# Products with values of two pairs of heads given out together, in the two layers with heads of 64

## The chip, the cores and the metric

The kernel runs on one core of a Trainium2 chip, alone. The metric is the device time of one execution in microseconds (us); the time before is the median of three runs. The engines are named as the profile names them: PE is TensorE (matrix products), PEld its loads of weights, DVE VectorE, ACT ScalarE, POOL GpSimd, SP the engine that issues most transfers.

## The reference

A decoder trunk of four layers over 256 positions and 1024 features, in float32. Layer by layer it does:

```
h = x
for i in range(4):                       # mixers: differential, MoBA, sliding window, differential
    h = h + mixer(rms_norm(h, attn_norm_g[i]))
    h = h + (max(rms_norm(h, mlp_norm_g[i]) @ w_up[i], 0) ** 2) @ w_down[i]
return rms_norm(h, final_norm_g)
```

Each mixer projects to queries, keys and values, turns a quarter of each head by rotary tables, and takes a softmax over masked scores; the products of the probabilities with the values go through an output projection. The differential layers have 8 heads with values of 128. The MoBA layer (i = 1) has 16 heads of 64; with 256 positions it holds a single block, so it is plain causal attention. The sliding-window layer (i = 2) has 16 query heads of 64 over 2 heads of keys and values, a window of 128, a bias, and a sink term in the denominator. These last two are the layers with heads of 64.

## The kernel before, in words

All activations stay in SBUF, transposed, as four tiles hT of 128 x 512. The weights are streamed: one DMA of 1 MB brings a raw piece (`fetch`, L66), ACT copies it to a rounded tile whi (`stage`, L80), DVE subtracts to get the rest, wlo (L81). `take` keeps two pieces staged ahead and five fetched ahead. A product with full precision is then made of several passes over the high and low parts.

The projections into a mixer are `proj` (L296, tile p_in). The attention works on pairs of heads, eight pairs in each of the two layers. For a pair n the steps are, by the name that the kernel's plan gives them:

- QK: queries and keys of two pairs are transposed on PE (L461, p_qk), and split into high and low parts by ACT (L470, L477) and DVE (L471, L478).
- SC: scores on PE (L271 to L273, tiles p_s0 and p_s1); masking with the row maximum on DVE (L336), exponentials on ACT (L339), in the sliding-window layer the sink terms (L342, L345); then the division by the sums (L424, L425, L427).
- TR: six transposes of the probabilities on PE (L354, p_t), brought to SBUF by ACT (L355, tile et).
- AV: the product with the values (L436, p_av). The two heads of a pair are two matrices of 64 columns, written to the two halves of one PSUM bank. This is four matmuls in the program and eight matmul instructions in the trace, each with its load of weights. ACT (L439) and DVE (L440) bring the result to the tile oo, in a high and a low part.

The output projection (p_d and p_e; L271 to L273 in the sliding-window layer, L605 and L606 in the MoBA layer) reads oo. PSUM tiles of the attention share four banks with the tag "wk", taken in turn: p_qk, p_s0, p_s1, p_t and p_av all rotate through them.

What sets the order: in the MoBA layer a written plan (L569 to L572), a list of thirteen entries; entry 2a is given out midway through projection a, entry 2a+1 after it, the last entry at the end. In the sliding-window layer the function `step` (L445): each call takes a new pair and advances the generators of the pairs in its line by one stage each. Whatever is given out is then placed by a scheduling layer, which may pull independent work, such as the matmuls of the output projection, between the steps; the order of the built program is what PE, ACT and DVE follow.

Of the kernel before, what the change touches and what calls it, by code (L numbers as in the profile page):

```python
# [39 lines left out]
def trunk(ctx: ExitStack, tc: tile.TileContext, xT, gains, lams, swa_row, fng, weights, out):  # L40
# [402 lines left out]
    line = []  # L443

    def step(block=None):  # L445

        line.append(block)
        full = len(line) > 3
        for x in line[:0:-1] + line[:1] if full else line[::-1]:
            if x is not None:  # L450
                next(x, None)
        if full:
            line.pop(0)

    def turn(src, n):

# [23 lines left out]
    def mixer_layer(i, n):  # L480
# [4 lines left out]
        if mixer == 2:  # L485
# [15 lines left out]
            for c in range(4):  # L501
                p = proj(n, (256, 1), False, first)
                qn = room(c % 2, [P, NT, 256], "qn")
                for t in range(NT):
                    for h in range(2):
                        s = slice(P * h, P * h + P)
                        o = qn[:, t, :].rearrange("p (b h e) -> p b h e", h=2, e=HD)[:, :, h, :]
                        bs = bias[:, 512 * h + P * c:512 * h + P * c + P]
                        V.scalar_tensor_tensor(o, p[t][:, s].rearrange("p (b e) -> p b e", e=HD), r[:, t:t + 1],
                                               bs.rearrange("p (b e) -> p b e", e=HD), op0=OP.mult, op1=OP.add)  # L510
                rope(qn[:, :, :].rearrange("p t (s e) -> p t s e", e=HD), 4)
                for do in second:
                    do()
                qs = []

                def block(b, c=c, qs=qs, qn=qn):
                    if b == 0:
                        qs += put_q(turn(lambda b, t: qn[:, t, P * b:P * b + P], 2))
                    h = 2 * c + b
                    step(head_block(  # L520
                        parts, [x[:, b] for x in qs], kT, lambda m: kv[:, m, P:2 * P], band,
                        [(sink[:, h + 8 * s:h + 8 * s + 1], nsink[:, h + 8 * s:h + 8 * s + 1]) for s in range(2)],
                        h,
                    ))

                first, second = [lambda f=block: f(0)], [lambda f=block: f(1)]
        else:
# [36 lines left out]
            def LAM(_):  # L564
                if i == 0:
# [1 line left out]

            order = (0, 1, "v", 2, 3, "v") if mixer else (0, 1, "v", 2, "v", 3)
            plan = [[], [], [(QK, 0), (LAM, 0), (SC, 0)], [(SC, 1)], [(TR, 0), (QK, 1), (SC, 2)], [(TR, 1), (SC, 3)],  # L569
                    [(TR, 2), (AV, 0)], [(TR, 3), (AV, 1)], [(AV, 2), (QK, 2), (OUT, 0), (SC, 4)], [(AV, 3), (SC, 5)],  # L570
                    [(TR, 4), (QK, 3), (OUT, 1), (SC, 6)], [(TR, 5), (SC, 7)],
                    [(AV, 4), (TR, 6), (AV, 5), (TR, 7), (AV, 6), (OUT, 2), (AV, 7), (OUT, 3)]]  # L572
            if mixer == 0:
                plan[8:] = [[(AV, 2), (QK, 2), (OUT, 0), (SC, 4)], [(AV, 3), (SC, 5)], [(TR, 4), (AV, 4)],
                            [(OUT, 1), (TR, 5), (AV, 5)],
                            [(QK, 3), (SC, 6), (SC, 7), (OUT, 2), (TR, 6), (AV, 6), (TR, 7), (AV, 7)]]
# [20 lines left out]
        for _ in range(3):  # L597
            step()
# [187 lines left out]
    for j in range(4):  # L786
        norm_sum(n, j)
    for i in range(DEPTH):
        parts, rest = mixer_layer(i, n)
        n = new_norm(gv[:, 1, i, :])  # L790
        (out_proj if i % 3 == 1 else out_proj_all)(parts, n, rest)
# [106 lines left out]
```

## Time and profile before

| | |
|---|---|
| median of 3 runs | 1148.51 us (1148.4 to 1148.52) |
| the profiled execution | 1148.08 us |
| its span, first to last instruction | 1146.0 us |
| mean granted TensorE clock | 0.998 |
| PE busy | 1135.6 us (99%) |
| PEld, DVE, ACT busy | 988.2, 827.8, 660.0 us |
| MoBA attention products (L436) | 64 matmul instructions, from 346.9 to 394.0 us |
| sliding-window attention products (L436) | 64 matmul instructions, from 623.4 to 657.3 us |

How to read it: a busy time is the union of an engine's instructions. Matmuls are pipelined, so each lasts longer than its share of the engine; what an instruction costs on PE is read from the distance between the starts of two neighbours. An "x8" in the timeline is a merged row of eight instructions.

### The profile page before, as it was taken

Reading aid. Unit: us, or ns where it says so; the run is one execution under the profiler, and the core shown is the slowest. Engines: PE = TensorE matmul, PEld = TensorE weight load, DVE = VectorE, ACT = ScalarE, POOL = GpSimd, SP = SyncE. Lnnn points to the kernel's source line nnn. Section 1 sums busy time; section 2 is a strip of 40 time slices with the busy share of each in tenths; the row PEclk is TensorE's granted clock in tenths of the full one; section 3 lists DMA queues with packets and bytes.
Section 4 is the critical chain, followed back from the end, with each engine's and each line's share of the span. In section 5 each row is a group of like instructions: output and inputs, shape, how many; then the busy total and the mean of one; then the engine's idle time right before and its main releaser. Section 6 shows DMA issues by size and latency. Waiting matters only on the chain.

```text
span 1146.0 us, 17054 instructions
## 1 busy us (share of the span) xinstructions
PE 1135.6 (99%) x6560; PEld 988.2 (86%) x6560; DVE 827.8 (72%) x1608; ACT 660.0 (58%) x1207; POOL 11.4 (1%) x39
## 2 busy tenths in 40 slices
PE   9999999999999999999999999999999999999997
PEld 7789888888887888888899898888888889888886
DVE  8978977656676698766569887775567788777454
ACT  6866656544476675554446756554447676665342
POOL 1000000000000000000000000000000000000000
PEclk9999999999999999999999999999999999999999
DMA  8543465555543355555563346555554444554551
GB/s 330 195 147 119 167 198 193 198 194 184 184 147 133 125 184 188 190 203 191 185 208 111 111 148 214 190 184 185 187 195 136 148 143 160 191 198 169 184 184 37
DMA packets 30609, 198.66 MB, mean 173 GB/s; under 512 B 3521, under 2 KB 5185, under 8 KB 7361
## 3 DMA queue, kind: packets, MB, share of 16 engines
q1 hardware_dynamic: 30240, 197.06, 50.2%
q8 instruction: 51, 0.84, 0.3%
q10 hardware_dynamic: 288, 0.52, 0.1%
q14 instruction: 30, 0.24, 0.1%
HBM read 196.52 MB, written 1.05 MB: 172 GB/s over the span
## 4 chain that ended last, share of the span: by engine, by line
PE 95%; DVE 2%; DMA 1%; ACT 1%; issue 0%; SPq 0%; DVEq 0%; ACTq 0%
PE p_up L605 20%; PE p_in L296 18%; PE p_down L605 15%; PE p_up L606 11%; PE p_down L606 8%; PE p_last L272 3%; PE p_last L271 3%; PE p_last L273 3%; PE p_d L272 2%; PE p_d L273 2%; PE p_d L271 2%; DMA raw<-in_weights 1%; PE p_t L354 1%; PE p_s L271 1%; PE p_qk L461 1%; PE p_av L436 1%
## 5 line engine op out<-in xcount | busy, mean ns | idle before, releaser
L81 DVE TENSOR_TENSOR wlo<-raw,whi 128x1024 fp32r<-128x1024 f32 (+1 forms) x374 | 447.2, 1209 | 204.1 <-ACT whi L80 203.3
L80 ACT ACTIVATE whi<-raw 128x1024 fp32r<-128x1024 f32 (+1 forms) x374 | 384.3, 1046 | 216.4 <-issue 111.1
L605 PE MATMUL p_up<-hg,whi 128*128 128x512 f32 x1024 | 356.7, 393 | 0.5 <-DVE hg L229 0.2
L606 PE MATMUL p_up<-hg,wlo 128*128 128x256 f32 x1024 | 285.5, 280 | 0.0
L605 PE MATMUL p_down<-uu,whi 128*128 128x512 f32 x768 | 266.4, 391 | 0.0
L605 PEld LDWEIGHTS p_up<-hg,whi 128*128 128x128 f32 x1024 | 191.4, 187 | 42.8 <-DVE hg L229 0.7
L606 PE MATMUL p_down<-uu,wlo 128*128 128x256 f32 x768 | 215.0, 280 | 0.0
L296 PE MATMUL p_in<-whi,hg 128*128 128x512 f32 (+1 forms) x736 | 211.6, 371 | 0.0
L606 PEld LDWEIGHTS p_up<-hg,wlo 128*128 128x128 f32 x1024 | 193.5, 189 | 0.5
L605 PEld LDWEIGHTS p_down<-uu,whi 128*128 128x128 f32 x768 | 143.6, 187 | 31.5
L296 PEld LDWEIGHTS p_in<-whi,hg 128*128 128x128 f32 x736 | 132.2, 189 | 23.3 <-DVE hg L229 0.8
L606 PEld LDWEIGHTS p_down<-uu,wlo 128*128 128x128 f32 x768 | 145.2, 189 | 0.0
L296 PE MATMUL p_in<-wlo,hg 128*128 128x512 f32 (+1 forms) x368 | 130.4, 369 | 0.1
L680 ACT ACTIVATE uu<-u 128x512 fp32r<-128x512 f32 x64 | 40.5, 633 | 71.1 <-DVE u L678 71.1
L296 PEld LDWEIGHTS p_in<-wlo,hg 128*128 128x128 f32 x368 | 68.8, 189 | 12.3 <-DVE wlo L81 1.4
L611 ACT ACTIVATE cross<-p_up 128x256 f32<-128x256 f32 x128 | 47.9, 374 | 39.3 <-PE p_up L606 33.8
L228 ACT ACTIVATE hg<-hT,gn 128x256 fp32r<-128x256 f32 x64 | 31.6, 502 | 65.5 <-DVE hT L624 65.3
L339 ACT ACTIVATE e<-ns,nm 128x128 f32<-128x128 f32 (+1 forms) x128 | 56.8, 446 | 11.6 <-DVE nm L336 11.2
L681 DVE TENSOR_TENSOR uu<-u,uu 128x512 fp32r<-128x512 f32 x64 | 44.2, 691 | 21.4 <-ACT uu L680 21.4
L272 PE MATMUL p_d<-oo,whi 128*128 128x256 f32 x192 | 55.3, 288 | 0.0
L271 PE MATMUL p_d<-oo,whi 128*128 128x256 f32 x192 | 55.2, 288 | 0.0
L612 DVE TENSOR_TENSOR relu<-p_up,cross 128x256 f32<-128x256 f32 x128 | 53.6, 419 | 1.5 <-ACT cross L611 1.5
(182 smaller groups left out, 1247.2 us busy)
## 6 DMA issues: line engine op xcount, KB each, us to landing
raw<-in_weights SPq DMA_DIRECT2D x181, 1024.0 KB, 4.9
raw<-in_weights SPq DMA_DIRECT2D x8, 256.0 KB, 4.6
raw<-in_weights SPq DMA_DIRECT2D x4, 512.0 KB, 6.8
hT<-in_xT SPq DMA_DIRECT2D x8, 128.0 KB, 4.4
bias<-in_swa_row SPq DMA_DIRECT2D x1, 512.0 KB, 4.6
grow<-in_fng SPq DMA_DIRECT2D x1, 512.0 KB, 3.7
out<-res SPq DMA_DIRECT2D x4, 128.0 KB, 2.1
out<-res ACTq DMA_DIRECT2D x2, 256.0 KB, 2.2
```

The source lines that it names most:

```text
L80: A.activation(hi[:, s], raw[:, s], AF.Copy)
L81: V.tensor_tensor(lo[:, s], raw[:, s], f(hi[:, s]), op=OP.subtract)
L271: T.matmul(out, lh, rh, start=start, stop=False, **kw)
L272: T.matmul(out, lh, rl, start=False, stop=False, **kw)
L273: T.matmul(out, ll, rh, start=False, stop=stop, **kw)
L296: T.matmul(out[t], n.both[k // 2][:, k % 2, x, P * t:P * t + P], r3(kb)(parts[k // kb][w])[:, k % kb, :], start=fresh, stop=k == 7 and x + ...
L339: A.activation(e[:, s], ns[:, s], AF.Exp, bias=nm[:, t:t + 1], scale=-1.0, accum_out=l[:, t:t + 1])
L605: T.matmul(r3(2)(p), hi, x, start=start, stop=False, skip_group_check=True)
L606: T.matmul(p[:, :S], lo, x[:, 0], start=False, stop=stop, skip_group_check=True)
L611: A.activation(cross, p[:, S:], AF.Copy)
L612: V.tensor_tensor(out, p[:, :S], cross, op=OP.add)
L681: V.tensor_tensor(both[:, :, 1], r3(2)(u), f(both[:, :, 0]), op=OP.subtract)
```

## The change

Only the order in which the steps of pairs are given out is changed, for the MoBA and the sliding-window layer. No instruction is added or removed there, and the plan of the differential layers stays as it was.

```diff
     def step(block=None):
         line.append(block)
-        full = len(line) > 3
-        for x in line[:0:-1] + line[:1] if full else line[::-1]:
-            if x is not None:
-                next(x, None)
-        if full:
-            line.pop(0)
+        if block is not None:
+            next(block)
+        if len(line) > 1 and line[-2] is not None:
+            next(line[-2])
+        if len(line) % 2 == 0:
+            for x in line[:-2]:
+                if x is not None:
+                    next(x, None)
+            line[:-2] = [None] * len(line[:-2])
...
-                    [(TR, 2), (AV, 0)], [(TR, 3), (AV, 1)], [(AV, 2), (QK, 2), (OUT, 0), (SC, 4)], [(AV, 3), (SC, 5)],
-                    [(TR, 4), (QK, 3), (OUT, 1), (SC, 6)], [(TR, 5), (SC, 7)],
-                    [(AV, 4), (TR, 6), (AV, 5), (TR, 7), (AV, 6), (OUT, 2), (AV, 7), (OUT, 3)]]
+                    [(TR, 2)], [(TR, 3), (AV, 0), (AV, 1)], [(QK, 2), (SC, 4)], [(AV, 2), (AV, 3), (SC, 5)],
+                    [(TR, 4), (QK, 3), (SC, 6)], [(TR, 5), (SC, 7)],
+                    [(AV, 4), (AV, 5), (TR, 6), (TR, 7), (AV, 6), (AV, 7)]]
             if mixer == 0:
+                plan[6:8] = [[(TR, 2), (AV, 0)], [(TR, 3), (AV, 1)]]
```

In the sliding-window layer a call of `step` now gives out the scores of the new pair and the transposes of the one before it; at every second call it also gives out the products of the two pairs that are older still. In the MoBA plan the products stand two by two: 0 and 1 after the third projection, 2 and 3 after the fourth, where they were at the ends of three stages, and 4 and 5, 6 and 7 in the last entry. OUT does nothing in these two layers. In the built program, PE's instructions of L436 then stand in eight runs of sixteen, four in each layer. Before, they stood in fifteen: fourteen of eight and, at the end of the MoBA layer, one of sixteen.

## The prediction

> **What bounds the kernel.** I read the page first: the busy shares, the slices, and the chain that ended last.
>
> ```profile
> span 1146.0 us, 17054 instructions
> PE 1135.6 (99%) x6560; PEld 988.2 (86%) x6560; DVE 827.8 (72%) x1608; ACT 660.0 (58%) x1207; POOL 11.4 (1%) x39
> ...
> PEclk9999999999999999999999999999999999999999
> ...
> PE 95%; DVE 2%; DMA 1%; ACT 1%; issue 0%; SPq 0%; DVEq 0%; ACTq 0%
> ```
>
> PE is busy in 99% of the span at full clock, and 95% of the chain is PE. A change pays only if it shortens what PE itself spends, start to start, or removes a wait of PE; it costs where PE now waits. Next I took the view of one source line, L436, the products with values.
>
> ```profile
> L436 PE MATMUL p_av<-et,v x64: 272/326/431, 346.9 to 394.0; 128*64 128x256 f32 x32, 128*64 128x128 f32 x32
> L436 PE MATMUL p_av<-et,rest x64: 272/326/431, 623.4 to 657.3; 128*64 128x256 f32 x32, 128*64 128x128 f32 x32
> ```
>
> The products use half of the array's columns each (128*64); everything around them is 128*128. The last view is the timeline of PE around these runs. In the MoBA layer there are seven runs (the first and the last are shown), in the sliding-window layer eight (likewise).
>
> ```profile
> 346.93 0.87 PE L436 MATMUL p_av<-et,v 128*64 128x256 f32 x8
> ...
> 391.90 0.82 PE L354 MATMUL p_t<-ident,e 128*128 128x128 f32 x6
> 392.65 1.57 PE L436 MATMUL p_av<-et,v 128*64 128x256 f32 x16
> 394.16 0.39 PE L606 MATMUL p_d<-oo,wlo 128*128 128x256 f32 x1
> 394.38 0.39 PE L605 MATMUL p_d<-oo,whi 128*128 128x512 f32 x1
> ...
> 623.41 0.87 PE L436 MATMUL p_av<-et,rest 128*64 128x256 f32 x8
> ...
> 656.23 0.38 PE L272 MATMUL p_d<-oo,whi 128*128 128x256 f32 x1
> 656.45 0.28 PE L273 MATMUL p_d<-oo,wlo 128*128 128x256 f32 x1
> 656.66 0.87 PE L436 MATMUL p_av<-et,rest 128*64 128x256 f32 x8
> 657.46 0.39 PE L271 MATMUL p_d<-oo,whi 128*128 128x256 f32 x1
> 657.68 0.28 PE L272 MATMUL p_d<-oo,whi 128*128 128x256 f32 x1
> 657.80 0.28 PE L273 MATMUL p_d<-oo,wlo 128*128 128x256 f32 x1
> ```
>
> Matmuls of 256 columns follow each other at 0.12 us (657.68 to 657.80). Around a run of half-width products they don't: the start before the run is 0.21 away from it (656.45 to 656.66), so entry costs 0.09; the first matmul behind the run holds its successor for 0.22 (657.46 to 657.68; likewise 394.16 to 394.38), so leaving costs 0.10. The run of eight lasts 0.80 from its first start to the next other matmul (656.66 to 657.46). A run of sixteen stands in this trace already, and lasts 1.51 (392.65 to 394.16), 0.09 less than two of eight.
>
> **Part one: the fewer runs.** Joining two runs takes off one entry, one leaving and that overhead inside: 0.09 + 0.10 + 0.09 = 0.28 us. In the built order of the changed kernel, fifteen runs become eight, three joins in the MoBA layer and four in the sliding-window layer. All of it is time of PE, which is the chain: 7 x 0.28 = 1.96 us saved, 0.84 and 1.12. The Trainium skill, TensorEngine Tiling (Array Packing), section Key Properties, says that a change of the tiling mode drains the engine; the trace agrees in kind. TensorE: Matmul & The Clock Gate, section Single matmul latency, puts a drain at about 175 ns; as an estimate, two drains for each of seven joins would be 2.45 us by that page.
>
> **Part two: what is moved.** No matmul, copy or DMA is new. The fetches, issued by SP, and POOL's instructions stand in the same order as before; ACT and DVE keep their instructions but not their order. The output projection's matmuls, which filled PE between single products, now stand elsewhere. So the cost, if any, is PE arriving at a wait that used to be met. One such wait of the trace gives the price:
>
> ```profile
> 619.71 0.28 PE L296 MATMUL p_in<-wlo,hg 128*128 128x256 f32 x1
> 619.83 0.28 PE L296 MATMUL p_in<-whi,hg 128*128 128x256 f32 x1
> 620.09 0.39 PE L271 MATMUL p_s<-kpadh,qhl 128*128 128x256 f32 x1
> 620.31 0.28 PE L272 MATMUL p_s<-kpadl,qhl 128*128 128x256 f32 x1
> ```
>
> The scores' first matmul comes 0.26 instead of 0.12 behind its neighbour, and the next 0.22 instead of 0.12 behind that: 0.14 late costs 0.24, the rest being a refill of the pipe.
>
> In the MoBA layer I find nothing late beyond what was. Products 0 to 3 move to a later place among projections that do not need them. At the end, products 4 and 5 run together, and the transposes of pair 6 follow them when they followed one product and some matmuls before. I take 0 there, with 0.24 as the upper end and a gain of 0.24 as the lower, since a wait there that is late now may go.
>
> The sliding-window layer is tighter. These rows are of one pair's round, and of ACT's queue:
>
> ```profile
> 630.07 0.37 ACT L439 ACTIVATE oo<-p_av 128x256 fp32r<-128x256 f32 x1
> 630.33 0.59 ACT L470 ACTIVATE qhl<-p_qk 128x512 fp32r<-128x512 f32 x1
> ...
> 631.08 0.28 PE L271 MATMUL p_s<-kpadh,qhl 128*128 128x256 f32 x1
> ...
> 637.34 0.95 DVE L427 TENSOR_TENSOR e<-e,rl 128x768 f32<-128x768 f32 x1
> 638.21 0.42 DVE L440 TENSOR_TENSOR oo<-p_av,oo 128x256 fp32r<-128x256 f32 x1
> 638.55 0.82 PE L354 MATMUL p_t<-ident,e 128*128 128x128 f32 x6
> 639.12 0.36 PE L272 MATMUL p_d<-oo,whi 128*128 128x256 f32 x1
> 639.32 0.28 PE L273 MATMUL p_d<-oo,wlo 128*128 128x256 f32 x1
> 639.62 0.87 PE L436 MATMUL p_av<-et,rest 128*64 128x256 f32 x8
> 640.42 0.66 PE L461 MATMUL p_qk<-ident,qn 128*128 128x128 f32 x4
> 640.83 0.36 PE L271 MATMUL p_d<-oo,whi 128*128 128x256 f32 x1
> ...
> 644.20 2.01 ACT L80 ACTIVATE whi<-raw 128x1024 fp32r<-128x1024 f32 x2 [1.77 <-PE p_d L272]
> ...
> 648.24 0.84 ACT L355 ACTIVATE et<-p_t 128x384 f32<-128x384 f32 x2
> ```
>
> Four places change their margin. First, the scores of pairs 4 and 6 wait for ACT's query copy L470, which now stands behind two copies L439. For pair 6 PE has only six output matmuls between p_qk and the scores: 0.41 (640.42 to 640.83), then 0.20 and five times 0.12, together 1.21 us from the start of p_qk; the copy can end 0.66 + 0.59 = 1.25 after it. That is late by 0.04, so 0.14 with the refill. For pair 4 the built order leaves eleven projection matmuls, 1.8 us, against 1.25 and what ACT has queued: near even. Second, the transposes of pairs 4 and 6 need the division L427. In the row it ended at 638.29 and the transposes began at 638.55, 0.26 to spare; in the built order two more masking steps stand before it on DVE, and for pair 4 a weight copy before its exponentials on ACT. Third, ACT now alternates halves of the weight copy L80 (2.01 for two, 1.0 each) with the two et copies of pairs 3 and 5 (0.42 each). The scores of pair 7 take the bank of the second of them: from the end of the first transposes ACT needs 0.42 + 1.0 + 0.42, plus about 0.6 of the weight copy it is in and of the matmul's end, 2.4; PE's work up to there (nine output matmuls, three transposes, five score matmuls) is about 2.3. Late by 0.1, so 0.2. Fourth, at the end TR 7 and its two products follow products 4 and 5 with nothing between; the second et copy and PE's arrival agree within 0.1.
>
> That is some six waits with margins between -0.2 and +0.2. None late costs 0; all late costs 6 x 0.24 = 1.44. I take three, 0.7, because the three that I could count out are late by little and a late one gives the next more time. The Trainium skill speaks against the change here: TensorEngine Tiling (Array Packing), section PSUM Bottleneck, says that tiling speeds up TensorE but not the emptying of PSUM. The rows bear it out: 0.37 on ACT and 0.42 on DVE for a product of 0.80.
>
> **The sum**: -1.96 + 0.7 = -1.26 us. The profiled execution is 1148.08 us, its span 1146.0, with 2.08 outside; it would become 1146.82. The median of the runs, 0.43 above it, would become 1147.25.
>
> **Rivals.** *All hidden*: every wait is met, -1.96, 1146.55. For it: PE's share of 99% shows a kernel in which nearly all waits are met already. Against: the margins above.
>
> *More than the joins*: late waits go too.
>
> ```profile
> 363.94 0.39 PE L296 MATMUL p_in<-wlo,hg 128*128 128x512 f32 x1
> 364.16 0.63 PE L296 MATMUL p_in<-whi,hg 128*128 128x512 f32 x2
> 364.67 0.62 PE L271 MATMUL p_s<-kpadh,qhl 128*128 128x256 f32 x2
> ```
>
> Where a product came third behind transposes its entry was 0.30 (639.32 to 639.62), 0.09 over the plain one; I count three such. The scores of pair 4 in the MoBA layer start 0.51 behind two matmuls that take 0.23 each, 0.05 late, 0.15 with the refill, and lose a copy ahead of them on ACT: -1.96 - 0.27 - 0.15 = -2.38, 1146.13. The drain of 175 ns by the Trainium skill's page (TensorE: Matmul & The Clock Gate) would bring it there too, since -2.45 gives 1146.06. Against it: the measured start-to-start distances are smaller than that.
>
> *Slower*: the sliding-window layer stops being bound by PE.
>
> ```profile
> 590.00:670.00 80.00, 79.66 (x629) 73.39 (x628) 63.60 (x195) 50.86 (x138) 0.75 (x2) 1.00 0.40 131
> ```
>
> One mechanism does it: ACT's queue in order. If a weight copy L80 that waits for a buffer (1.77 idle, above) stands before an et copy that PE's scores need, PE waits out the copy and then the exponentials, and the division comes that much later in each of the three rounds. At 1.5 us in each, 4.5 - 1.96 = +2.5, 1151.0. It decides once ACT's delay exceeds the work PE has between transposes and scores, about 2.3 us. Against: DVE is busy in 63.60 and ACT in 50.86 of these 80 us, so a round has slack to catch up.
>
> *Mostly spent*: six late waits, and longer than priced, between -0.5 and +2.3 us, 1147.9 for a typical one at -0.6. That the change doesn't do what it says is out: the built order shows the eight runs.
>
> **Numbers.** A difference of 0.2%, 2.3 us, is about what a measurement of this kernel can tell from no change. The forecast (between -0.5 and -1.9) has 0.42, all hidden 0.13, mostly spent 0.11: 0.66 within the bound. More than the joins 0.2, slower 0.14. The range holds the first four but for the ends of the last two: from -2.8 (1145.7) to +0.9 (1149.4).
>
> **What would show it.** In the profile after, L436 should stand in eight rows of x16, each about 1.51 from start to the next matmul; the MoBA layer should end some 0.8 us earlier, and the sliding-window layer's gain should be less than 1.1. Right or wrong on the waits shows in the timeline at the scores of pairs 4, 6 and 7 and the transposes of pairs 4 and 6: a distance of 0.2 to 0.5 ahead of them, then 0.22. The forecast is wrong if a run of sixteen takes 1.60 or more, or if PE waits over 0.5 us anywhere in the sliding-window layer.

## The result, and the profile after

| | before | after |
|---|---|---|
| median of 17 runs each | 1148.51 us (1147.99 to 1150.3) | 1146.44 us (1145.85 to 1147.19) |
| the profiled execution | 1148.08 us | 1146.28 us |
| its span | 1146.0 us | 1144.3 us |
| DVE, ACT busy | 827.8, 660.0 us | 827.9, 660.6 us |

The ratio of the runs is 0.998, with a 95% interval from 0.9973 to 0.9988. The medians differ by 2.07 us, 0.18%: a small gain, just under the bound of 0.2% that the prediction set itself, and more than the 1.26 that it forecast. The interval of the ratio means a gain of 1.4 to 3.1 us. The page of the changed kernel looks like the one before:

```profile
span 1144.3 us, 17044 instructions
PE 1133.7 (99%) x6560; PEld 987.0 (86%) x6560; DVE 827.9 (72%) x1608; ACT 660.6 (58%) x1207; POOL 11.4 (1%) x39
...
PEclk9999999999999999999999999999999999999999
...
PE 95%; DVE 2%; DMA 1%; ACT 1%; issue 0%; SPq 0%; DVEq 0%
```

PE carries the same 6560 matmuls and is still 95% of the chain, at the same clock. It is busy for 1.9 us less, and the span is 1.7 shorter. To see where, I cut the span at the first matmul of each MLP (tile p_up). These are its first rows in three layers, from the timeline of PE, of before and then of after:

```profile
119.25 0.50 PE L605 MATMUL p_up<-hg,whi 128*128 128x512 f32 x1
413.80 0.39 PE L605 MATMUL p_up<-hg,whi 128*128 128x512 f32 x1
667.11 0.47 PE L605 MATMUL p_up<-hg,whi 128*128 128x512 f32 x1 [0.22 <-DVE hg L229]
```

```profile
119.49 0.50 PE L610 MATMUL p_up<-hg,whi 128*128 128x512 f32 x1
412.80 0.39 PE L610 MATMUL p_up<-hg,whi 128*128 128x512 f32 x1
665.27 0.50 PE L610 MATMUL p_up<-hg,whi 128*128 128x512 f32 x1
```

From the first to the second start lies the MLP of layer 0 and the MoBA mixer: 294.55 before, 293.31 after, so -1.24. From the second to the third lies the sliding-window mixer: 253.31 and 252.48, so -0.83. Behind that the two traces agree to 0.1 us. The first start is 0.24 later in the trace after; over the profiles of all the kernels below it lies anywhere between 119.07 and 120.72, in a part of the program that is the same in all. So stages are compared here, not spans. The stage called MoBA and the stage called SW below are these two. Each is read from one profiled execution. Where kernels below share the order of a layer, their stages agree within 0.08 us (MoBA as changed: 293.31, 293.38, 293.34, 293.35; SW as before: 253.31, 253.30, 253.38).

The products stand in eight runs of sixteen; a join below means two shorter runs put together into one. These are the first run and the last two, with their neighbours, in the timeline of PE after:

```profile
353.28 1.52 PE L436 MATMUL p_av<-et,v 128*64 128x256 f32 x16
354.73 0.50 PE L296 MATMUL p_in<-whi,hg 128*128 128x512 f32 x1
...
651.35 1.52 PE L436 MATMUL p_av<-et,rest 128*64 128x256 f32 x16
652.81 0.87 PE L354 MATMUL p_t<-ident,e 128*128 128x128 f32 x6
653.61 1.57 PE L436 MATMUL p_av<-et,rest 128*64 128x256 f32 x16
655.12 0.38 PE L272 MATMUL p_d<-oo,whi 128*128 128x256 f32 x1
```

Start to next start, five of the eight take 1.45, the first among them (353.28 to 354.73). Two take 1.51, the last of each layer (653.61 to 655.12), and one 1.53, at 386.01, behind which the transposes of pair 6 are 0.08 late. The 1.51 that the prediction took for a run of sixteen was the time of one with a small wait in its middle: the one such run of before closes the MoBA layer, right behind the last transposes, where the run after also takes 1.51. In both, the first two pairs of instructions of the second product start 0.27 apart, 0.22 in the undisturbed runs.

A late start is a matmul that begins later behind its neighbour than the neighbour's own time. Two are large, and both are places that the prediction named:

```profile
640.21 0.66 PE L465 MATMUL p_qk<-ident,qn 128*128 128x128 f32 x4
640.62 0.36 PE L271 MATMUL p_d<-oo,whi 128*128 128x256 f32 x1
...
641.30 0.28 PE L273 MATMUL p_d<-oo,wlo 128*128 128x256 f32 x1
641.56 0.38 PE L271 MATMUL p_s<-kpadh,qhl 128*128 128x256 f32 x1
641.78 0.28 PE L272 MATMUL p_s<-kpadl,qhl 128*128 128x256 f32 x1
...
645.34 0.28 PE L272 MATMUL p_d<-oo,whi 128*128 128x256 f32 x1
645.62 0.50 PE L271 MATMUL p_s<-kpadh,qhl 128*128 128x512 f32 x1
645.95 0.40 PE L272 MATMUL p_s<-kpadl,qhl 128*128 128x512 f32 x1
```

The scores of pair 6 start 0.26 behind their neighbour instead of 0.12, the second score tile of pair 7 0.28, and the next matmul each time is about 0.10 late as well (0.22 instead of 0.12; 0.33 instead of 0.23): 0.24 and 0.26. Two more are late by 0.05 each. ACT's queue shows what the two large ones wait for:

```profile
639.68 0.39 ACT L439 ACTIVATE oo<-p_av 128x256 fp32r<-128x256 f32 x1
640.33 0.38 ACT L439 ACTIVATE oo<-p_av 128x256 fp32r<-128x256 f32 x1 [0.27 <-PE p_av L436]
640.90 0.60 ACT L474 ACTIVATE qhl<-p_qk 128x512 fp32r<-128x512 f32 x1 [0.20 <-PE p_qk L465]
642.80 1.06 ACT L80 ACTIVATE whi<-raw 128x1024 fp32r<-128x1024 f32 x1 [1.29 <-PE p_d L272]
643.76 0.47 ACT L355 ACTIVATE et<-p_t 128x384 f32<-128x384 f32 x1
644.13 1.05 ACT L80 ACTIVATE whi<-raw 128x1024 fp32r<-128x1024 f32 x1
645.08 0.48 ACT L355 ACTIVATE et<-p_t 128x384 f32<-128x384 f32 x1
```

The query copy (L474 now) ends at 641.50, and pair 6's scores start at 641.56. It wasn't held up by the two copies L439 ahead of it: ACT was idle for 0.20 until p_qk was there. What is short is PE's work between p_qk and the scores, six matmuls of the output projection where before fourteen stood. The et copy at 645.08 ends at 645.56, and pair 7's second score tile starts at 645.62. Here the alternation is just the predicted one: half of a weight copy, et, the other half, et.

### The profile page after: what moved, and what is told of

It reads as the page before. It is cut to its first block, busy times and chain, and to the rows that moved or that the text cites. A ratio compares the mean times of both kernels' runs of the same rounds, so it can differ in the third digit from the quotient of the medians.

```text
span 1144.3 us, 17044 instructions
## 1 busy us (share of the span) xinstructions
PE 1133.7 (99%) x6560; PEld 987.0 (86%) x6560; DVE 827.9 (72%) x1608; ACT 660.6 (58%) x1207; POOL 11.4 (1%) x39
## 4 chain that ended last, share of the span: by engine, by line
PE 95%; DVE 2%; DMA 1%; ACT 1%; issue 0%; SPq 0%; DVEq 0%
PE p_up L610 21%; PE p_in L296 18%; PE p_down L610 15%; PE p_up L611 11%; PE p_down L611 8%; PE p_last L273 3%; PE p_last L271 3%; PE p_last L272 3%; PE p_d L273 2%; PE p_d L272 2%; PE p_d L271 2%; PE p_t L354 1%; PE p_s L271 1%; PE p_qk L465 1%; DVE wlo L81 1%; PE p_av L436 1%
```

## The experiments

Theory: each run of half-width products costs PE a fixed time beside its products, so each join gains it; the late starts of the new order give part of that back, in the sliding-window layer. Rivals: the joins cost nothing or less, and the gain comes from waits that went; or the gain is not the runs' but that of the order around them.

### One layer at a time

The first kernel keeps `step` as it was before and has the new plan of the MoBA layer.

> The change in the MoBA plan alone, the sliding-window layer as before: three joins. If a join is worth 0.35 us wherever it stands (theory: price of a run), the MoBA layer, from the first product of the up-projection before it to the one behind it, shortens by 1.2 us against before, and the sliding-window layer not at all; the run is 1.0 to 1.3 us faster than before. If the gain comes from where the other work was put (rival: placement), it needs both parts and this shows under 0.6 us.

The second keeps the old plan and has the new `step`.

> The change in the sliding-window layer alone, the MoBA plan as before: four joins. Price of a run: 4 x 0.33 = 1.3 us off, less the late waits ahead of the scores of pairs 5, 6 and 7 (0.04, 0.24, 0.05 and 0.26, together 0.6) that the new order brings: 0.7 to 0.9 us faster than before, all of it in that layer. Placement: no gain, or a gain without the late waits.

| | median | ratio to before | MoBA | SW |
|---|---|---|---|---|
| MoBA layer alone | 1146.95 us | 0.9985 (0.9976 to 0.9994) | -1.17 | -0.01 |
| sliding-window layer alone | 1147.66 us | 0.9991 (0.9982 to 1.0) | +0.07 | -0.88 |
| both (the change) | 1146.44 us | 0.998 (0.9973 to 0.9988) | -1.24 | -0.83 |

The last columns are the stages against those of before. By the stages the two parts add: nothing that the change does in one layer is paid in the other, and each layer's gain alone is within 0.07 of its gain in the whole. The medians are too coarse to show this: against the 1148.78 us of before that goes with them, the two kernels are 1.83 and 1.12 us faster, together more than the change, each with an interval about 2 us wide, and the second interval reaches 1. The kernel with the sliding-window layer alone has the same late starts, to 0.01 us (0.14 and 0.10 at the scores of pair 6, 0.16 and 0.10 at pair 7), so they belong to the order and not to one execution.

### More joins: two runs of thirty-two in each layer

```diff
-        if len(line) % 2 == 0:
-            for x in line[:-2]:
+        if len(line) in (5, 9):
+            for x in line[:-1]:
...
-                    [(TR, 2)], [(TR, 3), (AV, 0), (AV, 1)], [(QK, 2), (SC, 4)], [(AV, 2), (AV, 3), (SC, 5)],
+                    [(TR, 2)], [(TR, 3)], [(AV, 0), (AV, 1), (AV, 2), (AV, 3), (QK, 2), (SC, 4)], [(SC, 5)],
...
-                    [(AV, 4), (AV, 5), (TR, 6), (TR, 7), (AV, 6), (AV, 7)]]
+                    [(TR, 6), (TR, 7), (AV, 4), (AV, 5), (AV, 6), (AV, 7)]]
```

> Two runs of 32 instructions in each of the two layers in place of four of 16: four more joins. Price of a run: 4 x 0.34 = 1.4 us less than the changed kernel, if PE meets its waits. Rival (emptying of PSUM): four products fill all four banks of the attention, and what follows on PE waits for ACT and DVE, 0.37 and 0.42 us for each product; then it is 0 to 3 us slower than the changed kernel, with late waits at the transposes and scores behind the run.

1147.45 us, ratio 0.9988 (0.9979 to 0.9997). The intervals of this kernel and the change overlap, but its two stages are together 1.23 us longer than those of the change, although it has four runs fewer. The MoBA stage gained another 0.31: two more joins, less two new late starts of 0.13 and 0.16 ahead of transposes and one of 0.04 at the scores of pair 4. The sliding-window stage lost 1.54. Three of the four runs take 2.75 from start to the next matmul. The fourth has a wait inside, and PE waits in front of it:

```profile
628.54 0.28 PE L296 MATMUL p_in<-whi,hg 128*128 128x256 f32 x1
629.08 0.39 PE L271 MATMUL p_s<-kpadh,qhl 128*128 128x256 f32 x1 [0.27 <-ACT qhl L473]
...
629.90 0.52 PE L273 MATMUL p_s<-kpadh,qhl 128*128 128x256 f32 x2
631.15 0.85 PE L354 MATMUL p_t<-ident,e 128*128 128x128 f32 x6 [0.73 <-DVE e L427]
```

DVE's timeline of the same kernel says why the division L427 is late:

```profile
626.46 2.35 DVE L81 TENSOR_TENSOR wlo<-raw,whi 128x1024 fp32r<-128x1024 f32 x2
628.73 0.15 DVE L345 TENSOR_TENSOR l<-l,es 128x4 f32<-128x4 f32 x1
629.06 0.69 DVE L474 SCALAR_TENSOR_TENSOR qhl<-p_qk,qhl 128x512 fp32r<-128x512 f32 x1 [0.17 <-ACT qhl L473]
...
630.05 0.95 DVE L427 TENSOR_TENSOR e<-e,rl 128x768 f32<-128x768 f32 x1
```

Two weight subtractions stand ahead of the sums, then the rest of the query copy, and then the division, which ends at 631.00. In the changed kernel the same division ends at 631.01, and the next transposes start only at 631.69: nothing waits for it. There, a run of sixteen products stands ahead of p_qk (626.90, 1.45 us). Taken away from here, that work isn't there to cover the 1.4 us (0.42 and 0.10 at the scores, 0.88 at the transposes) by which PE is now early. The loss has the size that the rival in the expectation gives, but what is waited for is the query copy, the division and, inside the run, an et copy (it ends at 634.35, and the fourth product's weights are loaded from 634.40), not the emptying of a bank. The rival named *slower* in the prediction is of this kind, at a queue in order, but with DVE in ACT's part.

### The same products one call later

```diff
-        if len(line) % 2 == 0:
-            for x in line[:-2]:
+        if len(line) % 2 == 1:
+            for x in line[:-3]:
...
```

> The changed kernel with the pairs of products in the sliding-window layer given out one call later, behind the transposes and splits of the next queries: the query copy L470 no longer stands behind two copies L439. If that order makes the scores of pair 6 late (0.24), this wait goes, and the layer shortens by 0.24 against the changed kernel, by 0.5 if the wait ahead of pair 7 goes too and by another 0.3 for the last two runs, which now join. Rival: the waits come from the weight copies L80 between the et copies; then the 0.24 at pair 6 stays or another wait takes its place, and the layer is as long as or longer than the changed kernel's.

1148.64 us, ratio 1.0003 (0.9994 to 1.0011): the gain is gone, where 0.24 or more beyond the change had been expected. The MoBA stage is 293.34; the sliding-window stage 254.88, 2.4 above that of the change, with as many runs in the layer as there (16, 8, 8 and 32). The stall is in the same place, at the scores (0.42 late), at the transposes behind them, and again at the next pair's scores:

```profile
631.63 0.85 PE L354 MATMUL p_t<-ident,e 128*128 128x128 f32 x6 [0.71 <-DVE e L427]
...
634.89 0.50 PE L271 MATMUL p_s<-kpadh,qhl 128*128 128x512 f32 x1 [0.25 <-ACT et L355]
```

With the number of runs held, the order alone costs 2.4 us: a product that is given out later no longer covers PE's wait. Both kernels together show that the order decides as much as the joins do.

### The products ahead of the transposes

```diff
         if block is not None:
             next(block)
-        if len(line) > 1 and line[-2] is not None:
-            next(line[-2])
         if len(line) % 2 == 0:
             for x in line[:-2]:
                 if x is not None:
                     next(x, None)
             line[:-2] = [None] * len(line[:-2])
+        if len(line) > 1 and line[-2] is not None:
+            next(line[-2])
```

> The changed kernel with the two products given out ahead of the transposes of the newest pair at every second call of the sliding-window layer, not behind. Price of a run: the first pair of products stands apart again here, so one entry and leaving more (0.2 to 0.35); the query copy stays behind two copies, so the wait of 0.24 ahead of pair 6 stays unless the transposes in between give it time. Between 0.3 shorter and 0.5 longer than the changed kernel's layer.

1146.22 us, ratio 0.9982 (0.9974 to 0.9991). The sliding-window stage is 252.38, 0.10 below the change. It has one run more: the first two stay apart, in runs of eight with four matmuls between them. But one late start of 0.05 and 0.10 is all that is left, where the change has 0.60:

```profile
645.13 0.28 PE L272 MATMUL p_d<-oo,whi 128*128 128x256 f32 x1
645.25 0.28 PE L271 MATMUL p_s<-kpadh,qhl 128*128 128x256 f32 x1
...
645.61 0.28 PE L273 MATMUL p_d<-oo,wlo 128*128 128x256 f32 x1
645.72 0.39 PE L271 MATMUL p_s<-kpadh,qhl 128*128 128x512 f32 x1
```

Pair 7's scores come 0.12 behind their neighbours, as all met waits do. 0.45 of waits gone and one join given up leave 0.10: by that the join is worth about 0.35. This is rough, since the wait ahead of the MLP is 0.09 longer here than in the change, and the MLP of layer 1 itself 0.07 shorter.

### Fewer joins: products cut in halves

In the old order of both layers, each of the products 0 to 3 of the MoBA layer is given out in two halves, its 256-column matmuls and its 128-column ones, with other work between.

```diff
         for m, cols in ((0, slice(0, S)), (1, slice(P, S))):
+            if m and halves:
+                yield
...
+                    [(TR, 2), (AV, 0)], [(AV, 0), (TR, 3), (AV, 1)], [(AV, 1), (QK, 2), (SC, 4), (AV, 2)], [(AV, 2), (SC, 5), (AV, 3)],
+                    [(AV, 3), (TR, 4), (QK, 3), (OUT, 1), (SC, 6)], [(TR, 5), (SC, 7)],
```

> The kernel before with products 0 to 3 of the MoBA layer cut into their two halves (first and second key block), given out at different entries of the plan: the same instructions in twelve runs in place of seven. Price of a run: entry 0.09 and leaving 0.10 for each further run, some of the inner 0.15 too: 5 x 0.2 to 0.34 = 1.0 to 1.7 us longer in the MoBA layer. Placement: no change, as no work is added.

1150.15 us, ratio 1.0013 (1.0004 to 1.0022): slower. The medians differ by 1.37, as expected; the MoBA stage lost 2.08, more than expected. Twelve runs stand there instead of seven, four from the halves and one that the scheduling layer made:

```profile
354.50 0.65 PE L438 MATMUL p_av<-et,v 128*64 128x256 f32 x4
355.08 0.50 PE L296 MATMUL p_in<-whi,hg 128*128 128x512 f32 x1
...
360.75 0.44 PE L438 MATMUL p_av<-et,v 128*64 128x128 f32 x4
361.12 1.09 PE L463 MATMUL p_qk<-ident,qk 128*128 128x128 f32 x8
...
365.02 0.65 PE L438 MATMUL p_av<-et,v 128*64 128x256 f32 x2
365.60 0.39 PE L272 MATMUL p_s<-kpadl,qhl 128*128 128x256 f32 x1
```

A whole product is 0.80; its halves are 0.58 and 0.37 (354.50 to 355.08, 360.75 to 361.12), together 0.15 more. That is the part of the fixed cost that lies inside a run. It lies at the run's two ends: in the run at 353.28 of the changed kernel, the second pair of instructions starts 0.27 behind the first where later pairs of 256 columns take 0.22, and the next matmul starts 0.21 behind the last pair where earlier pairs of 128 columns take 0.11. Half of product 2 was parted between its two heads (at 365.02 and 366.50), and each part of two instructions takes as long as four did. The two instructions of a part start 0.27 apart; the two that use the array's two column halves start 0.007 apart, in every other run of this kernel. Five more runs at 0.34 make 1.70, and the 0.43 of products that ran one after the other instead of side by side make 2.13. Counted in the two traces, the distances at the borders and inside the runs grew by 2.05. That the stage grew by nearly the same, 2.08, is partly luck: late starts of 0.36 that the kernel before had at scores and transposes are gone, and the 113 matmuls of the output projection behind the last run take 20.01 instead of 19.64 without a wait. Why they do is open.

### Full width

The products on the whole array (128 columns, twice the work, into a wider PSUM tile), in the changed kernel's order: the output of each product is 128 rows of which the copies take the half that is wanted.

```diff
-                T.matmul(p[r, cols], v(m)[:, r], ets[c][:, S * m:S * m + S - P * m], start=(m == 0), stop=(m == 1),
-                         skip_group_check=True)
+                T.matmul(p[:, S * c + P * m:S * c + S], v(m), ets[c][:, S * m:S * m + S - P * m],
+                         start=(m == 0 and c == 0), stop=(m == 1), skip_group_check=True)
```

> The changed kernel with the products on the whole width of the array: both heads' values as 128 columns of weights, one head's probabilities at a time, so that half of each result is not used; the copies to oo take the two halves one by one. If entry and leaving cost because the array changes from whole to half width (theory), a run now begins 0.12 or 0.23 us behind its neighbour and the next matmul follows at its usual distance. If they cost because any run of another kind breaks the stream (rival), entry stays 0.2 to 0.32 and leaving 0.22. The run itself is longer, since the two heads no longer share the array: 4 x 0.21 + 4 x 0.11 = 1.3 in place of 0.65 to 0.8 for a pair, some 8 us for sixteen pairs, less the 8 entries and leavings of 0.19.

1155.7 us (two runs), ratio 1.0065 (1.0046 to 1.0083). What it was made for are the borders of a run:

```profile
368.08 0.39 PE L296 MATMUL p_in<-wlo,hg 128*128 128x512 f32 x1
368.31 0.39 PE L296 MATMUL p_in<-whi,hg 128*128 128x512 f32 x1
368.54 2.78 PE L436 MATMUL p_av<-et,v 128*128 128x256 f32 x16
371.07 0.36 PE L271 MATMUL p_s<-kpadh,qhl 128*128 128x256 f32 x1
371.27 0.28 PE L272 MATMUL p_s<-kpadl,qhl 128*128 128x256 f32 x1
```

The run starts 0.23 behind a matmul of 512 columns, which is that matmul's own time (368.08 to 368.31): entry is free. The last product holds its successor only 0.03 where its neighbours of the same 128 columns stand 0.11 apart, and the successor then holds the next 0.20 instead of 0.12: the two cancel, so leaving is free too. Nothing extra lies inside: sixteen instructions take 0.22 each for the eight of 256 columns and 0.11 for the eight of 128, 2.62, less those 0.08. Six of the eight runs start so; the other two start 0.30 behind a matmul of 256 columns, 0.05 after an et copy has ended (631.23 and 659.06), so they wait. So the fixed cost belongs to the half width, not to the products or the order. The full width changes the loads of weights along with the matmuls, and no run here tells which of the two costs it. The kernel's loss is 4.68 and 4.78 us in the two stages against the change, 9.5 in all where 6.5 had been expected. Eight products without the shared array are 8 x (1.31 - 0.65) = 5.3 us more in each, and the four runs cost 1.4 less, which makes 3.9; of the 0.8 that is left, 0.5 in the MoBA layer is one wait for an et copy, and about 0.5 in the sliding-window layer are the two late starts just named, 0.18 each with 0.10 behind it. The cause of the rest is open.

### Joining where a cover is left, and both together

Of the two joins that the plan with thirty-twos adds in the MoBA layer, this kernel makes only the first: products 0 to 3 in one run, by the first of the two plan lines in that diff.

> The changed kernel with products 0 to 3 of the MoBA layer in one run of 32, the tail as in the changed kernel. Price of a run: one more join, 0.34 off the MoBA layer, less the late wait ahead of the scores of pair 4 (0.15) if the four copies L439 stand before its query copy. So 0.2 to 0.35 shorter than the changed kernel. Rival (emptying): no gain or a loss.

1146.08 us, ratio 0.9982 (0.9973 to 0.9991). The stage is 293.27, 0.04 below the change, not the expected 0.2 to 0.35. The join was made:

```profile
358.97 2.82 PE L436 MATMUL p_av<-et,v 128*64 128x256 f32 x32
361.72 1.09 PE L465 MATMUL p_qk<-ident,qk 128*128 128x128 f32 x8
```

2.75 for thirty-two is 0.15 less than two of 1.45. But the scores of pair 4 are 0.04 late again, with 0.10 behind it, as they were before the change, where the change has 0.08 there. That is 0.06 of the missing 0.3. The rest stands behind the last run, in the output projection:

```profile
393.35 0.39 PE L611 MATMUL p_d<-oo,wlo 128*128 128x256 f32 x1
413.00 0.40 PE L610 MATMUL p_up<-hg,whi 128*128 128x512 f32 x1
```

Up to the first of these rows this kernel is 0.39 ahead of the change (393.35 - 119.73 against 393.50 - 119.49). Between the two rows, 111 matmuls take 19.65, and the same 111 take 19.30 in the change: each pair of 512 and 256 columns takes 0.353 instead of 0.347, with no wait. Only the kernel with the products cut in halves shows the same. So up to there the join gained about what was expected, and 0.36 was lost in a part that was not touched; the cause of that is open.

The last kernel takes the best order of each layer: the MoBA plan of the thirty-twos, and the products ahead of the transposes.

> Both layers in the order that was best by itself: the MoBA layer with two runs of 32 (293.00 us there, against 293.31 in the changed kernel), the sliding-window layer with products given out ahead of the next transposes in five runs of 8, 8, 16, 16, 16 (252.38 against 252.48). If a stage's time belongs to its own order, as theory one has it (joined runs of half-width products at 0.34 us each, less the late waits of that order), the two gains add: MoBA layer 293.0, sliding-window layer 252.4, profiled execution 0.4 us below the changed kernel's 1146.28, that is 1145.9, and a ratio to before of 0.998. If the layers lend to each other (the MoBA layer's late end shifting the weight copies of the sliding-window layer), one of the stages keeps its old time or loses: 1146.2 or more. If joins cost nothing once they are all made, the rival's case, 1146.3.

1145.85 us (1145.37 to 1147.04), ratio 0.9977 (0.9968 to 0.9986), 2.86 us below its before of 1148.71. The stages are 292.98 and 252.41, each what it was by itself, 0.40 in all below the change. So the gains of the two layers add. Its profiled execution took 1146.97, not the expected 1145.9: the first MLP starts at 120.72 there, 1.23 later than in the trace of the change. By the ratios this is the fastest kernel here, but its interval overlaps that of the change; that it is faster is shown by the stages alone.

## Why the prediction was right, and where it was off

**What bounds the kernel** was right: what PE lost, start to start, is what the time lost, and no change of DVE's or ACT's order mattered but where PE waited.

**The joins were undersized.** The term was 0.09 to enter, 0.10 to leave and 0.09 inside, 0.28 for each. Entry and leaving held, but for runs with transposes behind them, where leaving costs 0.03 to 0.06. The inside was read from the one run of sixteen that before has, and that run holds a wait of 0.05 (1.505 where undisturbed ones take 1.45). Runs of 8, 16 and 32 take 0.80, 1.45 and 2.75: that is 0.15 and 0.65 for each eight. So the inside is 0.15 and the whole 0.34, and seven joins are 2.38 where the prediction had 1.96. That is 0.42 of the 0.81 by which the sum fell short. The products cut in halves show the same 0.15, and the full width shows that it goes with the half width. The Trainium skill, TensorEngine Tiling (Array Packing), section Key Properties, has a drain at each change of mode; the trace agrees in kind, since each run costs a fixed time. The estimate of 2.45 us that the prediction worked out with the 175 ns of the Trainium skill, TensorE: Matmul & The Clock Gate, section Single matmul latency, lies nearer to the 2.38 than the rows that I chose. No run here shows a drain as such, only 0.09, 0.15 and 0.10 in three places.

**The late starts were well sized, by a partly wrong list.** 0.7 was taken for the sliding-window layer as three waits of six at 0.24; the trace has 0.24 and 0.26, and two of 0.05, 0.60 in all. That the totals agree is in part luck. Pair 6's scores were named with a price of 0.14; they are 0.14 late and cost 0.24. What sets them is p_qk and its copy in a row, as in the prediction's arithmetic, and not the two copies L439 that its words put ahead; the chain takes 1.35 from the start of p_qk (640.21 to 641.56) where 1.25 was counted. Pair 7's were named with 0.2 and cost 0.26, by the mechanism named. The scores of pair 4 and the transposes of pairs 4 and 6 are on time. So neither the premise of *all hidden*, that every wait is met, nor that of *mostly spent*, that all six are late, holds.

**The sum**, stage by stage. By layer the prediction had -0.84 for MoBA and -1.12 + 0.7 = -0.42 for the sliding window; measured are -1.24 and -0.83, so each is short by 0.4. Sliding window: four joins, -1.36; +0.60; +0.05 for the wait in the last run; the entry of one product that was late by 0.08 and isn't, and 0.09 of the wait ahead of the MLP, -0.17: together -0.88, measured -0.83 and -0.88. MoBA: three joins, -1.02; late starts -0.14 and +0.08 at the scores of pair 4, and -0.07 and +0.08 at the transposes of pair 6, which before came 0.04 late (388.10) with 0.03 behind it; together -1.07, measured -1.24 and -1.17. Of the rest, 0.05 is the run ahead of the transposes of pair 6, which leaves at 0.03 and not at 0.10. About 0.1 is spread over distances that differ by less than 0.02 each; its cause is not shown. The prediction put the MoBA waits at 0, with a gain of 0.24 as one end.

**The rival that came nearest** in number is *all hidden*, at 1146.55 against the measured 1146.44, nearer than the forecast of 1147.25. That is luck: it had no new wait and cheap joins, and the runs show waits of 0.60 and dearer joins, which nearly cancel. *More than the joins*, at 1146.13, has the same 2.38 that seven joins are worth, by another way: it let late waits go and kept 0.28 for a join. In the runs a join is worth more, and of the waits more came than went.

**The median** moved by 2.07, the profiled execution by 1.80. The two stages moved by 2.07 together, and the start of the program is 0.24 later in the profiled execution after. That the median moved by just as much as the stages is chance, since its interval is 1.7 us wide.

## What to carry to other kernels

A run of matmuls that use half of the array's columns cost PE about 0.34 us beside its products in this kernel, for runs of 4 to 32 instructions, so put such runs together, and keep the two matmuls that share the array next to each other. A product that waits for its partner is also work that PE no longer has in front of a wait: before moving it, count what PE has left up to each result that ACT or DVE must bring. Two of these orders, with as few runs or fewer, made the sliding-window layer longer than before the change, by 0.7 and 1.6 us. Read a fixed cost from several lengths, not from one pair: a single long run held a wait.

## What had not been expected of the hardware

A late start often costs twice: behind the scores named above that were 0.04 to 0.42 late (but for the two of 0.05 right behind transposes), the next matmul was 0.10 late too, for first matmuls of 256 and of 512 columns. Behind transposes that were 0.88 late it was 0.03. And the sharing of the array is all of the half width's gain: two instructions on different column halves start 0.007 us apart, so a run of four took 0.58; two on the same half start 0.27 apart, and took 0.58 alone.
